# Low-rank products of an RWKV-7 mixer: half-height weights against full-height weights padded with zeros

## The chip, the cores and the metric

The kernel runs on one core of a Trainium2 chip. The metric is the device time of one execution in microseconds (us), as the median of three runs. A difference counts from about 0.2% (2.1 us) on.

## The reference, cut to what matters

One layer of a hybrid decoder: RMSNorm, one input projection of 512 tokens from 2048 to 7824 columns, three mixers side by side (RWKV-7, block attention, gated linear attention), an output projection, a residual and a last RMSNorm, all in float32. The change is in the RWKV mixer, in the two low-rank products that make the decay and the in-context rate of every token:

```python
r, k, v, wd, ad = _split(p, RWKV_SHIFT_SIZES)      # wd, ad: (512 tokens, 64)
w = w0 + jnp.tanh(wd) @ w2                          # w2: (64, 1024)
w = -jax.nn.softplus(-w) - 0.5
decay = jnp.exp(-jnp.exp(w))
a = jax.nn.sigmoid(a0 + ad @ a2)                    # a2: (64, 1024)
```

The contraction is over 64. The result is 1024 columns wide, in eight tiles of 128 (a tile is a pair of heads).

## The kernel before, in words

TensorE's fast float32 type (float32r) keeps fewer bits than float32. The kernel therefore splits an operand into a part hi, rounded to float32r, and a rest lo, and adds up several products. The input projection takes for each tile of 128 output columns 16 blocks of 128 input columns, and for each block three products of 128x128 weights with 512 tokens: hi by h hi, hi by h lo, lo by h hi (line 120, function mmr). They go to the four PSUM banks gb. A unit is four blocks, so 12 products. Its weights are loaded by SyncE's DMA queue into one of three buffers raw, rounded by ScalarE into hi (line 173) and subtracted by VectorE into lo (line 133), up to three units ahead of TensorE. The output projection is built in the same way.

Everything else (the three mixers) is side work: Python generators, resumed between the products of the projection when a rough model of the engines' queues says that their operands are there. That fixes, at build time, one order of instructions for each engine. The side work uses four other PSUM banks, sb.

The low-rank products are in `pair_decay`, called eight times, once for each pair of heads. The tokens' side is stored split on both halves of the 128 partitions: `wd` has tanh's hi part in partitions 0 to 63 and its lo part in 64 to 127, and `ad` has the lo part in 0 to 63 and the hi part in 64 to 127. The weights' side has w2's columns (and a2's) on both halves. So one 128-row product `w2hi` by `wd` gives hi·hi + hi·lo. What is left, the weights' lo part by the tokens' hi part, is a product over 64 rows: partitions 0 to 63 for the decay, 64 to 127 for the rate. Both lo parts share one tile, `w2lo`. Then ScalarE takes the sigmoid of each bank into `s0` (named vT in the profile) and `s2` (part of scr).

Tiles near it: `wl2` holds the split weights of the job "low" (16 columns of the gated linear attention's gate) and 96 columns of zeros behind them, since every "low" product reads 128 columns from its own place. `stat` and `rst` are small tiles with sums of squares and inverse roots, used at the start and in the last norm; `gn` holds the group norm's statistics of the RWKV mixer.

Of the kernel before, what the change touches and what calls it, by code (L numbers as in the profile page):

```python
# [9 lines left out]
F32 = mybir.dt.float32  # L10
F32R = mybir.dt.float32r
# [14 lines left out]
# first columns of the parts of w_in  # L26
# [4 lines left out]
# columns of the per-partition parameters  # L31
P_NW, P_MU, P_W0, P_A0, P_KK, P_KA, P_RK, P_LW, P_LB, P_GB, P_GN = 0, 16, 41, 49, 57, 65, 73, 81, 89, 97, 99
NPAR = 100
# columns of the constants
# [4 lines left out]
# the tiles of 128 columns of the input projection, in the order in which they are computed  # L39
# [22 lines left out]
class Clock:  # L62
    """A rough model of the engines' queues, used only to choose the order of emission."""
# [29 lines left out]
def tile_hybrid(ctx: ExitStack, tc: tile.TileContext, x, xT, wu, wlow, wout, par, cst, w2a2_d, aup_d, fw, out):  # L93
# [8 lines left out]
    def sb(name, shape, dt=F32, tag=None):  # L102
        t_ = pool.tile(list(shape), dt, name=name, tag=tag or name)
        return t_
# [91 lines left out]
    stat = sb("stat", [128, 4, 4])  # L196
    rst = sb("rst", [128, 8])
    wd = sb("wd", [128, S], F32R)
    ad = sb("ad", [128, S], F32R)
    wl2 = sb("wl2", [128, KT * 32 + 96], F32R)  # L200
# [14 lines left out]
    # RWKV: four heads (two pairs) at a time  # L215
# [12 lines left out]
    gn = sb("gn", [128, 3, 16])  # L228
    pbuf = [sb(f"pbuf{i}", [128, S + 1]) for i in range(2)]
# [9 lines left out]
    # the parts that live where others have been used up  # L239
# [7 lines left out]
    # the lanes of the triangular solves, once the rest of the preparation is over  # L247
# [7 lines left out]
    # the transposed x, before the branches start  # L255
# [39 lines left out]
    def pump():  # L295
        """Resume the side work whose operands are there by now."""
        for s in list(sides):
            now = ck.t["pe"]
            if runnable(s) and s.ready + MARGIN <= now and ck.t["dve"] < now + BACKLOG and ck.t["act"] < now + BACKLOG:
                resume(s)  # L300
        sides[:] = [s for s in sides if not s.done]

    def force(flag, what):
        """Let the tensor engine wait until the side work has got to flag."""
        while not flag():
            ready = [s for s in sides if runnable(s)]
            if not ready:
                raise RuntimeError(f"stuck: {what}: {[s.name for s in sides]}")
            s = min(ready, key=lambda s: s.ready)
            ck.t["pe"] = max(ck.t["pe"], s.ready + MARGIN)  # L310
            resume(s)
            sides[:] = [s for s in sides if not s.done]
# [44 lines left out]
    def rsqrt(v, r, scale, e):  # L357
        """r = (v scale + e)^-1/2"""
        ts(v, v, scale, e, ALU.mult, ALU.add)
        n = numel(v)  # L360
        ck.add("pool", 0.1 + 0.17 * n)
        nc.gpsimd.tensor_tensor(r, v, mhalf[:, 0:n], op=ALU.pow)  # L362
        yield None
# [41 lines left out]
    def resets(t):  # L405
        """1, and 0 where a chunk starts"""
        ck.add("pool", 1.0)
        nc.gpsimd.memset(t, 1.0)
        nc.gpsimd.memset(t[:, 0:S:C], 0.0)
# [3 lines left out]
    def parts(src):  # L413
        """src in two parts that add up to it exactly, each of them float32r"""
        yield lambda: not lock[0]
        lock[0] = True
        act(xr[0], src, AF.Copy)
        tt(xr[1], src, xr[0].bitcast(F32), ALU.subtract)
        yield None

    def pair_decay(pr, j):
        resets(s4)
        act(w2hi, w2a2, AF.Copy)
        yield None
        tt(w2lo[0:64], w2a2[0:64, 0:128], w2hi[0:64, 0:128].bitcast(F32), ALU.subtract)
        tt(w2lo[64:128], w2a2[64:128, 128:256], w2hi[64:128, 128:256].bitcast(F32), ALU.subtract)
        if pr < 7:
            load_w2a2(pr + 1)
        yield None
        b = yield from bank()  # L430
        mmr(sbk[b], w2hi[:, 0:128], wd, True, False)
        mmr(sbk[b], w2lo[0:64], wd[0:64], False, True)
        act(s0, sbk[b], AF.Sigmoid, bias=col(P_W0, pr))
        release(b)
        b = yield from bank()
        mmr(sbk[b], w2hi[:, 128:256], ad, True, False)
        mmr(sbk[b], w2lo[64:128], ad[64:128], False, True)
        act(s2, sbk[b], AF.Sigmoid, bias=col(P_A0, pr))
        release(b)
        yield None  # L440
        ck.add("dve", 1.15)
        nc.vector.tensor_tensor_scan(s1, s4, s0, 0.0, ALU.mult, ALU.add)
        yield None
        act(Pb[:, :, 1:C + 1], s1.rearrange("p (c t) -> p c t", t=C), AF.Exp, scale=-DECAY)
        act(s0, s1, AF.Exp, scale=DECAY)
        yield None
# [63 lines left out]
    def a_stage(q, c):  # L510
        """the products within chunks c and c + 1; the two heads of a pair take different row tiles and so banks"""
        mi = mask_i[:, None, None, :].to_broadcast([128, 2, 2, C])
        ms = mask_s[:, None, None, :].to_broadcast([128, 2, 2, C])
        bs = yield from bank(2)
        pa, pb = (sbk[b].rearrange("p (c r n) -> p c r n", c=2, r=2) for b in bs)
        for i in range(2):
            for j in range(2):
                mm(pa[:, i, j], BK[0:64, c + i, j], AW[0:64, c + i, j, 0:2])
                mm(pb[:, i, j], BK[64:128, c + i, j], AW[64:128, c + i, j, 1:3])
        yield None  # L520
        cs = slice(c, c + 2)
        act(Lt[0:64, :, cs], pa[0:64, :, :, 0:64].rearrange("p c r t -> p r c t"), AF.Copy)
        act(Lt[64:128, :, cs], pb[64:128, :, :, 64:128].rearrange("p c r t -> p r c t"), AF.Copy)
        yield None
        flags[f"L{q}"] = flags.get(f"L{q}", 0) + 1
        tt(ARB[:, cs, :, 0], pa[:, :, :, 64:128], mi, ALU.mult)
        tt(AW[64:128, cs, :, 0], pa[64:128, :, :, 0:64], ms[64:128], ALU.mult)
        release(bs[0])
        yield None
        tt(ARB[:, cs, :, 1], pb[:, :, :, 0:64], mi, ALU.mult)  # L530
        tt(AW[0:64, cs, :, 2], pb[0:64, :, :, 64:128], ms[0:64], ALU.mult)
        release(bs[1])
        flags[f"A{q}"] = flags.get(f"A{q}", 0) + 1
        yield None
# [12 lines left out]
    def key_norms(q, j):  # L547
        """the squared norms of the unnormalised keys of a token, laid out as the lanes of solve()"""
# [25 lines left out]
    def solve():  # L574
        """Tt: -(diag(n2) + L)^-1, transposed; one diagonal block of 32 per lane, then the block beside them."""
# [55 lines left out]
    def y_pair(q, cp):  # L631
        """the mix of chunks 2 cp and 2 cp + 1, tokens on the partitions"""
# [23 lines left out]
    def chain(q):  # L656
# [3 lines left out]
        for c in range(NC):  # L660
# [22 lines left out]
            if c < NC - 1:  # L683
# [7 lines left out]
                if c >= 2:  # L691
                    # the state that is overwritten has been read
                    yield lambda: flags.get(f"ymm{q}", 0) > (c - 2) // 2
# [92 lines left out]
    def by_chunks(src, parts):  # L786
        """Transposes src: head h's columns of every chunk of tokens to the half h of the partitions."""
# [13 lines left out]
    def gla(g):  # L801
# [64 lines left out]
        vt = [fb[(4, 7)[i]].rearrange("p (c n) -> p c n", n=128) for i in range(2)]  # chunks 0 to 3, 4 to 7  # L866
# [64 lines left out]
    def moba(h):  # L931
# [5 lines left out]
        def window(w, p, pT):  # L937
            """128 queries: their scores, the softmax over the keys so far, its product with the values"""
# [112 lines left out]
    # the operands of the last pass take the place of the branches' tiles  # L1051
# [41 lines left out]
    def square(n, r):  # L1093
        """the sum of squares of x"""
# [35 lines left out]
    def advance(u):  # L1130
        """Emit the loads and splits for the units up to u."""
# [32 lines left out]
    nc.vector.tensor_copy(wl2[:, KT * 32:], att.rearrange("p a t -> p (a t)")[:, 0:96])  # L1164
# [79 lines left out]
    for cb in range(3):  # L1244
        banks = oldest if cb % 2 == 0 else sbk
        order = [(n, tb) for n in range(KT) for tb in range(4)]
        if cb == 0:
            # the bank of the input projection's last job comes last
            order[:8] = [(0, 0), (0, 1), (0, 2), (1, 0), (1, 1), (1, 2), (0, 3), (1, 3)]
# [17 lines left out]
    # the last columns: the blocks of tokens end one after the other  # L1267
# [5 lines left out]
    def scaled(tb):  # L1273
        """the rows of the block of tokens, times the inverse root of their mean square"""
# [28 lines left out]
def arrange(inputs):  # L1303
    """The arrays of the launch: the inputs, laid out for the loads, and constants that depend on shapes alone."""
# [22 lines left out]
    # for every pair of heads the columns of w2 and of a2, on both halves of the partitions  # L1327
# [29 lines left out]
```

## Time and profile before

| | |
|---|---|
| median of 3 runs | 1071.08 us (1071.03 to 1071.57) |
| span of the profiled execution, first to last instruction | 1069.9 us |
| TensorE (PE) busy | 1044.7 us, 98% of the span |
| VectorE (DVE), ScalarE (ACT), GpSimd (POOL) busy | 62%, 42%, 7% |
| share of PE in the chain of work that ended last | 89% |

The page gives no time of the profiled execution other than its span; the median of the runs lies 1.2 us above that span. PE's busy time adds up modelled ends of pipelined products (a 128x512 product is shown as 0.39 us while the next one begins 0.23 us after it), so the steps between starts tell more than the durations.

### The profile page before, as it was taken

What the parts mean: (1) busy time and instruction counts of PE and PEld (TensorE: products, weight loads), DVE (VectorE), ACT (ScalarE), POOL (GpSimd) and SP (SyncE); (2) the same over time, 40 slices, a digit from 0 to 9 for tenths busy, and PEclk for the clock granted to TensorE, in tenths of its full rate; (3) what the DMA queues carried; (4) which work ended last, traced back from release to release, by engine and by line L of the source; (5) the groups of instructions that cost most, each with busy time, mean ns of one, the idle gap of its engine ahead of it and who ended that gap; (6) DMA issues with size and microseconds to landing.
All of it is one profiled execution on the core that took longest, in us unless ns stands there. A gap on an engine that the chain in (4) does not pass through costs nothing.

```text
span 1069.9 us, 16750 instructions
## 1 busy us (share of the span) xinstructions
PE 1044.7 (98%) x6376; PEld 819.0 (77%) x6376; DVE 667.7 (62%) x1345; ACT 444.6 (42%) x789; POOL 71.9 (7%) x73
## 2 busy tenths in 40 slices
PE   7799999999999999999999999999999999899996
PEld 5577888767778886777887777788877787688885
DVE  6646669656856885676778665667955564434343
ACT  6464543343454433235534423545322354423333
POOL 4500000000100000000000001000000000102020
PEclk9899999999999999999999999999999999999999
DMA  7232333412233342223334222333341245543434
GB/s 248 94 90 86 89 89 99 108 57 83 80 104 90 100 113 71 70 82 112 94 94 118 66 70 74 85 98 100 105 103 51 80 148 168 177 154 94 164 119 157
DMA packets 80400, 111.87 MB, mean 105 GB/s; under 512 B 28208, under 2 KB 29424, under 8 KB 80192
## 3 DMA queue, kind: packets, MB, share of 16 engines
q1 hardware_dynamic: 80176, 109.76, 34.7%
q8 instruction: 50, 0.82, 0.3%
q0 software_dynamic: 144, 1.05, 0.3%
q14 instruction: 30, 0.25, 0.1%
HBM read 98.62 MB, written 12.16 MB: 104 GB/s over the span
## 4 chain that ended last, share of the span: by engine, by line
PE 89%; DMA 3%; DVE 2%; ACT 2%; issue 2%; POOL 2%; SPq 0%; ACTq 0%; POOLq 0%; DVEq 0%
PE gb L120 67%; PE sb L116 11%; PE sb L120 10%; PE sb L125 2%; POOL f L1103 2%; DVE scr L133 1%; DMA raw<-in_wout_dram 1%; DVE lo L133 1%; DMA raw<-mix 1%; ACT hhi L173 1%; DMA Ld<-Lt 0%; ACT hi L173 0%; DMA raw<-in_wu_dram 0%; ACT f L173 0%; DMA scr<-Ld 0%
## 5 line engine op out<-in xcount | busy, mean ns | idle before, releaser
L120 PE MATMUL gb<-hhi,hi 128*128 128x512 f32 x976 | 404.6, 415 | 6.3 <-ACT hi L173 6.3
L120 PE MATMUL gb<-hhi,lo 128*128 128x512 f32 x976 | 383.7, 393 | 0.8 <-DVE lo L133 0.8
L120 PE MATMUL gb<-hlo,hi 128*128 128x512 f32 x976 | 383.0, 392 | 0.0
L173 ACT ACTIVATE hi<-raw 128x512 fp32r<-128x512 f32 x296 | 186.1, 630 | 398.7 <-PE gb L120 274.7
L133 DVE TENSOR_TENSOR lo<-raw,hi 128x512 fp32r<-128x512 f32 x296 | 213.1, 723 | 213.4 <-ACT hi L173 210.3
L120 PEld LDWEIGHTS gb<-hhi,hi 128*128 128x128 f32 x976 | 184.3, 189 | 51.5 <-ACT hi L173 6.5
L120 PEld LDWEIGHTS gb<-hhi,lo 128*128 128x128 f32 x976 | 184.1, 189 | 42.0 <-DVE lo L133 1.9
L120 PEld LDWEIGHTS gb<-hlo,hi 128*128 128x128 f32 x976 | 184.7, 189 | 33.7 <-issue 1.0
L133 DVE TENSOR_TENSOR scr<-scr 64x30 f32<-64x30 f32 (+14 forms) x240 | 77.5, 323 | 7.2
L120 PE MATMUL gb<-hi,hhi 128*128 128x512 f32 x128 | 50.2, 392 | 2.4 <-ACT hi L173 2.4
L120 PE MATMUL gb<-lo,hhi 128*128 128x512 f32 x128 | 50.2, 392 | 0.4 <-DVE lo L133 0.4
L120 PE MATMUL gb<-hi,hlo 128*128 128x512 f32 x128 | 49.9, 390 | 0.0
L173 ACT ACT_TABLE_LOAD x34 | 43.6, 1283 | 1.0 <-DVE VS L153 0.4
L153 DVE COPY VS<-sb 64x128 f32<-64x128 f32 x64 | 18.5, 288 | 33.5 <-PE sb L116 32.4
L173 ACT ACTIVATE Lt<-sb 64x256 f32<-64x256 f32 (+1 forms) x64 | 19.3, 327 | 33.0 <-PE sb L116 30.4
L362 POOL TENSOR_TENSOR gn<-gn,mhalf 128x16 f32<-128x16 f32 x4 | 12.0, 2995 | 307.1 <-DVE gn L149 307.1
L173 ACT ACTIVATE f<-sb 64x256 f32<-64x256 f32 (+3 forms) x52 | 17.3, 363 | 35.9 <-PE sb L125 19.1
L120 PE MATMUL sb<-lo,hhi 128*128 128x512 f32 x80 | 31.2, 390 | 0.0
L120 PE MATMUL sb<-hi,hlo 128*128 128x512 f32 x80 | 31.2, 390 | 0.0
L120 PE MATMUL sb<-hi,hhi 128*128 128x512 f32 x80 | 31.2, 389 | 0.0
L120 PEld LDWEIGHTS gb<-hi,hhi 128*128 128x128 f32 x128 | 24.0, 188 | 8.1 <-ACT hi L173 3.2
L120 PE MATMUL sb<-late,hhi 128*128 128x512 f32 x96 | 30.0, 394 | 0.0
(229 smaller groups left out, 1145.8 us busy)
## 6 DMA issues: line engine op xcount, KB each, us to landing
raw<-in_wu_dram SPq DMA_DIRECT2D x244, 256.0 KB
raw<-in_wout_dram SPq DMA_DIRECT2D x64, 256.0 KB
raw<-mix SPq DMA_DIRECT2D x16, 256.0 KB
f<-in_x_dram SPq DMA_DIRECT2D x16, 256.0 KB
Ld<-Lt SPq DMA_DIRECT2D x4, 512.0 KB
mix<-f SPq DMA_DIRECT2D x8, 256.0 KB
mix<-ARB SPq DMA_DIRECT2D x8, 256.0 KB
AW<-in_xT_dram SPq DMA_DIRECT2D x6, 256.0 KB
```

What stands on the lines that cost most here:

```text
L116: nc.tensor.matmul(o, l, r, start=start, stop=stop)
L120: nc.tensor.matmul(o, l, r, start=start, stop=stop)
L125: nc.tensor.transpose(o, i, ident[:k, :k])
L133: nc.vector.tensor_tensor(o, a, b, op=op)
L153: nc.vector.tensor_copy(o, a)
L173: nc.scalar.activation(o, a, f, **kw)
L362: nc.gpsimd.tensor_tensor(r, v, mhalf[:, 0:n], op=ALU.pow)
L1103: nc.gpsimd.tensor_tensor(fb[0], fb[0], fb[1 + m % 3], op=ALU.add)
```

## The change

The lo part of a2 gets a place of its own, `a2lo`, the 128 columns behind the "low" weights in `wl2` (96 before). `w2lo` and `a2lo` are filled with zeros once, at the start, by two VectorE copies where there was one. Each pair then writes its lo parts into the same 64 partitions as before, so the other 64 stay zero, and the two lo products take all 128 partitions of weights and tokens. `stat` and `rst` now lie inside `gn`. Comments were removed. Apart from the one copy that is added on VectorE at the start, the instructions of all engines stand in the same order as before.

```diff
     wd = sb("wd", [128, S], F32R)
     ad = sb("ad", [128, S], F32R)
-    wl2 = sb("wl2", [128, KT * 32 + 96], F32R)
+    wl2 = sb("wl2", [128, KT * 32 + 128], F32R)
+    a2lo = wl2[:, KT * 32:KT * 32 + 128]
...
-    stat = sb("stat", [128, 4, 4])
-    rst = sb("rst", [128, 8])
...
     gn = sb("gn", [128, 3, 16])
+    stat = gn[:, 0].rearrange("p (t c) -> p t c", t=4)
+    rst = gn[:, 1, 0:8]
...
     def pair_decay(pr, j):
...
-        tt(w2lo[64:128], w2a2[64:128, 128:256], w2hi[64:128, 128:256].bitcast(F32), ALU.subtract)
+        tt(a2lo[64:128], w2a2[64:128, 128:256], w2hi[64:128, 128:256].bitcast(F32), ALU.subtract)
...
         mmr(sbk[b], w2hi[:, 0:128], wd, True, False)
-        mmr(sbk[b], w2lo[0:64], wd[0:64], False, True)
+        mmr(sbk[b], w2lo, wd, False, True)
...
         mmr(sbk[b], w2hi[:, 128:256], ad, True, False)
-        mmr(sbk[b], w2lo[64:128], ad[64:128], False, True)
+        mmr(sbk[b], a2lo, ad, False, True)
...
-    nc.vector.tensor_copy(wl2[:, KT * 32:], att.rearrange("p a t -> p (a t)")[:, 0:96])
+
+    for z in (a2lo, w2lo):
+        nc.vector.tensor_copy(z, att.rearrange("p a t -> p (a t)")[:, 0:128])
```

## Rows read from the trace of the kernel before

**Rows 1.** The page's busy time, share of the span and instructions.
```profile
PE 1044.7 (98%) x6376; PEld 819.0 (77%) x6376; DVE 667.7 (62%) x1345; ACT 444.6 (42%) x789; POOL 71.9 (7%) x73
```
**Rows 2.** Chain that ended last: start, length, engine, output, line, count.
```profile
929.92 43.52 PE sb L120 x192
```
**Rows 3.** Timeline, first pair: start, length, engine, line, operation, tiles [idle before <-releaser].
```profile
67.28 0.40 PE L120 MATMUL gb<-hhi,lo 128*128 128x512 f32 x1
67.28 0.19 PEld L120 LDWEIGHTS sb<-wd,w2hi 128*128 128x128 f32 x1
67.51 0.40 PE L120 MATMUL sb<-wd,w2hi 128*128 128x512 f32 x1
67.84 0.18 PEld L120 LDWEIGHTS sb<-wd,w2lo 64*128 64x128 f32 x1 [0.37 <-issue]
67.84 0.49 PE L120 MATMUL sb<-wd,w2lo 64*128 64x512 f32 x1
...
68.26 0.50 PE L120 MATMUL sb<-ad,w2hi 128*128 128x512 f32 x1
68.37 0.69 ACT L173 ACTIVATE vT<-sb,params 128x512 f32<-128x512 f32 x1 [1.63 <-PE sb L120]
...
68.69 0.50 PE L120 MATMUL sb<-ad,w2lo 64*128 64x512 f32 x1
...
69.12 0.50 PE L120 MATMUL gb<-hhi,hi 128*128 128x512 f32 x1
...
69.23 0.69 ACT L173 ACTIVATE scr<-sb,params 128x512 f32<-128x512 f32 x1 [0.17 <-PE sb L120]
69.46 0.39 PE L120 MATMUL gb<-hlo,hi 128*128 128x512 f32 x1
```
**Rows 4.** Instructions that touch w2lo: count, minimum/median/maximum ns, first and last start.
```profile
L120 PE MATMUL sb<-wd,w2lo x8: 492/492/502, 67.8 to 690.7; 64*128 64x512 f32 x8
...
L120 PE MATMUL sb<-ad,w2lo x8: 491/498/498, 68.7 to 691.5; 64*128 64x512 f32 x8
```
**Rows 5.** Timeline, third pair, which comes behind 64-row products.
```profile
220.85 0.50 PE L120 MATMUL gb<-hhi,hi 128*128 128x512 f32 x1
221.19 0.39 PE L120 MATMUL gb<-hlo,hi 128*128 128x512 f32 x1
...
222.13 0.50 PE L120 MATMUL sb<-wd,w2hi 128*128 128x512 f32 x1
...
224.17 0.39 PE L120 MATMUL gb<-hlo,hi 128*128 128x512 f32 x1
```
**Rows 6.** Timeline, the recurrence beside the third pair.
```profile
222.25 0.59 DVE L153 COPY VS<-sb 64x128 f32<-64x128 f32 x2 [0.73 <-PE sb L116]
...
225.35 0.45 PE L116 MATMUL sb<-VS,BKt 128*64 128x64 f32 x8
```
**Rows 7.** Timeline, eighth pair, with 128x128 products right behind it.
```profile
690.36 0.39 PE L120 MATMUL sb<-wd,w2hi 128*128 128x512 f32 x1
...
691.95 1.16 PE L116 MATMUL sb<-att,f 128*128 128x128 f32 x8
```
**Rows 8.** Who waited for whom: us in total, times, longest.
```profile
ACT hi L173 <- PE gb L120: 274.7, 142, 9.5
```
**Rows 9.** Timeline, VectorE at the start.
```profile
2.91 0.20 DVE L1164 CAST wl<-att 128x96 fp32r<-128x96 f32 x1
...
4.96 0.75 DVE L139 SCALAR_TENSOR_TENSOR hlo<-AW,params,hhi 128x512 fp32r<-128x512 f32 x1 [1.85 <-ACT hhi L173]
```
**Rows 10.** Windows: busy us (instructions) of each engine, PEclk, DMA share, GB/s.
```profile
900.00:920.00 20.00, 18.26 (x79) 14.31 (x77) 7.33 (x11) 7.41 (x12) 0.00 (x0) 1.00 0.63 199
```
**Rows 11.** Windows of PE alone, around the stretch at the lower clock.
```profile
40.00:42.00 2.00, 1.24 (x6) 0.50 0.00 0
...
46.00:48.00 2.00, 2.00 (x7) 0.50 0.00 0
48.00:50.00 2.00, 2.00 (x11) 0.92 0.04 12
```

## Prediction, made before the changed kernel ran

> **What bounds the kernel now.** I read the page first, then the chain that ended last, the waits, and then the timeline at each of the eight places that the change touches. The page has TensorE (PE) busy for 98% of the span [rows 1], but that figure adds up modelled ends that overlap, so it doesn't say whether PE runs at its pace. The distance between starts does. Where nothing disturbs it, the chain has 192 products of 128x512 in 43.52 us [rows 2], that is 0.227 us from one start to the next. This step is the unit of everything below. The other engines mostly wait for PE: ScalarE alone waits 274.7 us, in 142 places, for a product to be through with a weight buffer before it can write the next one [rows 8]. So in the input projection a step that PE saves is a step that the end comes earlier, unless something that is now just in time becomes late.
>
> The eight calls of the low-rank products are two half-height products each, from 67.8 us to 691.5 us [rows 4]. Look at the first call [rows 3]. The full-height product `w2hi` by `wd` starts 0.23 us after its predecessor, though it writes another bank with other weights; its weight load starts at 67.28 us, together with the product before it. Then the pace breaks. The load of `w2lo` (marked 64*128) doesn't start beside the product before it but together with its own product, after 0.37 us in which the load path stood idle for "issue", that is, for nothing that the profile shows. From start to start the trace has 0.33 us to the first lo product, 0.42 us to `ad` hi, 0.43 us to the second lo product, 0.43 us to the next main product (67.51, 67.84, 68.26, 68.69, 69.12), and 0.34 us to the one after it (69.46). Each change between 128 and 64 rows costs about 0.1 us on the step into it and as much on the step behind it; in the middle, where every step has both, it is 0.2 us. The columns that are streamed are 512 in all of them, so the half height buys nothing.
>
> The Trainium skill, "TensorEngine Tiling (Array Packing)", Key Properties, says that a change of the tiling mode, other than a change of the tile within a mode, drains TensorE. The trace agrees: four changes in a call, and 0.81 us over the undisturbed pace.
>
> **The change part by part.**
>
> *The two lo products take 128 rows.* Then all four products of a call, and the main products around them, have one height. I take 0.227 us for each step, as for the other full-height products: half of the weights being zero changes neither the 512 columns nor the 128 of the load. No row has a full-height product with such operands, but a full-height product into an sb bank is in rows 3 (`w2hi` by `wd`, a step of 0.23 us). The bounds of this unknown: 0.227 us from below, since no 128x512 product in the trace is closer to its predecessor, and from above the 0.43 us of now, which would mean no gain. I take the lower one, because the row of a full-height product into sb gives it.
>
> Per call, from the start of `w2hi` by `wd` to the second product behind the call:
> - Four calls (first, second, fourth, seventh) stand between main products. Five steps take 1.95 us (67.51 to 69.46) and would take 5 x 0.227 = 1.135 us: 0.815 us less each, 3.26 us.
> - Two calls (third, fifth) come directly behind small side products of another height. Five steps take 2.04 us (222.13 to 224.17) [rows 5]. The entry out of the small products stays: 0.34 us, as from 220.85 to 221.19 in the same rows. So 0.34 + 4 x 0.227 = 1.25 us: 0.79 us less each, 1.58 us.
> - Two calls (sixth, eighth) are followed by 128x128 products. Four steps take 1.59 us (690.36 to 691.95) [rows 7] and would take 0.91 us: 0.68 us less each, 1.36 us. The small products behind them no longer come out of a half-height one; by the 0.11 us of the step 69.12 to 69.46 that is up to 0.2 us more for the two, which I leave to the range.
>
> Sum: 3.26 + 1.58 + 1.36 = 6.2 us.
>
> *The zeros.* One more copy on VectorE at the start, and one a third wider. The old copy took 0.20 us [rows 9]; two of 128 columns are about 0.45 us together, 0.25 us more. VectorE stands idle for 1.85 us right behind, until ScalarE has the first part of h [rows 9]. So it costs nothing. Without that cover it would cost 0.25 us.
>
> *a2lo behind the "low" weights, and stat and rst in gn.* The last "low" products read 128 columns, so their tail now reads `a2lo` instead of zeros, into rows of the bank that nobody uses. In the order of the instructions these products stand between the first and the second call, so both the write before and the write after them have long distances. The group norm is through with `gn` before the output projection writes the sums of squares there. No new wait here; from 0 to 0.1 us.
>
> *What then comes late.* ScalarE's two sigmoids are 0.69 us each and stand 0.86 us apart [rows 3]. The first can start some 0.2 us earlier (0.1 us from the step, 0.1 us from a product shown as 0.40 instead of 0.49 us). The second then waits for the first, no longer for PE, and ends about 0.3 us earlier, while PE gets 0.8 us ahead. So ScalarE loses 0.5 us of its lead in each call. Its lead is up to three units of twelve products, 36 x 0.227 = 8 us, and it has idle time to make it up [rows 8]. Beside the third call runs the recurrence: VectorE's copies of VS end at 222.84 us, and the product that needs them starts at 225.35 us [rows 6]. Of these 2.5 us the call takes 0.8 us, so they still arrive in time. Between 900 and 920 us PE idles 1.7 us for data [rows 10]; the loads there are released by buffers that PE frees, so this stretch moves forward as a whole.
>
> From the span of the profiled execution, 1069.9 - 6.2 = 1063.7 us. The median of the runs is 1.2 us above that span, so the predicted time is 1064.9 us, 0.58% less. Measurement tells about 0.2% (2.1 us) from no change.
>
> **The rivals.**
>
> *The steps don't shrink.* The 0.43 us steps could belong to the four products and not to their height, for instance to changing weights and bank. Then the time stays at 1071.1 us. Against it stands the 0.23 us step into the first product of the call, which changes both. Half of it is possible: at 0.34 us for each of the 16 products in place of 0.227 us, 1.8 us of the gain are lost and the time is 1066.7 us.
>
> The Trainium skill has a rule by which it would come out this way: "TensorE: Matmul & The Clock Gate", Part 3, The mechanism, says that a weight load overlaps with a running product only when its row group differs. By that rule full-height loads would never overlap, each step would stay at some 0.42 us (a load of 0.19 us and a step of 0.23 us), and the time would be 1071.1 us. The trace disagrees: full-height loads start beside a running full-height product, and it is the half-height load that does not.
>
> *PE's lead is eaten.* If after each call PE had to wait for ScalarE, it would keep 0.3 of its 0.8 us, so 2.3 to 2.6 us in all, and the time is 1068.6 us. For it: the sigmoids do become a queue of two. Against it: ScalarE's long waits for PE.
>
> *Slower: the clock.* PE ran at the lower of its two levels (1.2 GHz, granted clock 0.50) from when it resumed in the slice of 40 to 42 us until the slice of 48 to 50 us [rows 11], behind the idle time at the start, which cost about 8 us x 0.5 = 4 us. The change shifts VectorE's first instructions and with them possibly that stretch, or a later one. It decides from 12.4 us of work at the lower level on, when it takes more than the 6.2 us. Two further stretches of 8 us would take 8 us: 1072.9 us. Against it: the idle time of rows 9 covers the shift, and nothing in the change makes PE idle.
>
> **How the numbers follow.** The forecast, with its part where a step is not fully won (1064 to 1067.2 us): 0.85. PE's lead eaten for the most part (1067.5 to 1069 us): 0.06, of which nearly all still counts as faster. Steps don't shrink, by whatever cause: 0.06. Slower: 0.03. Faster by over 0.2% is 0.85 + 0.05 = 0.90; within 0.2% 0.06 + 0.01 = 0.07; slower 0.03. The Trainium skill's rule on row groups is one such cause; I give it 0.02 of the 0.06. The range goes from 1063.9 us (6.4 us saved, and the 0.5 us by which runs of one kernel differ) to 1067.2 us (the steps half won, with the same scatter).
>
> **What would show it.** In the profile after, the four products of each call and the two main products behind them start 0.23 us apart, their loads are marked 128*128 and have no idle time of "issue" before them, and the first call is over by about 68.65 us instead of 69.46 us. The last call lies some 5.5 us earlier, and from there to the end the distance stays the same. The forecast is wrong if the steps stay above 0.3 us, if PE shows new waits for ScalarE in the 10 us behind a call, or if the slices at the lower clock change in number.

## The result, and the profile after

| | before | after |
|---|---|---|
| median of 4 runs each | 1071.05 us (1071.0 to 1071.57) | 1065.52 us (1063.7 to 1066.36) |
| span of the profiled execution | 1069.9 us | 1064.5 us |

The ratio is 0.995, with a 95% interval of 0.9936 to 0.9964. The forecast was 1064.9 us, 0.6 us under the median. Two further measurements, each beside the kernel before on its own chip, gave 0.9946 (0.9932 to 0.9961) and 0.9948 (0.9935 to 0.996).

The first call after, as the timeline shows it for TensorE and the weight loads of the two lo products (columns as in [rows 3], to which these rows answer; `a2lo` lies in `wl2` and is called wl in the profile):

```profile
67.06 0.39 PE L120 MATMUL sb<-wd,w2hi 128*128 128x512 f32 x1
67.06 0.19 PEld L120 LDWEIGHTS sb<-wd,w2lo 128*128 128x128 f32 x1
67.28 0.40 PE L120 MATMUL sb<-wd,w2lo 128*128 128x512 f32 x1
...
67.52 0.40 PE L120 MATMUL sb<-ad,w2hi 128*128 128x512 f32 x1
67.52 0.19 PEld L120 LDWEIGHTS sb<-ad,wl 128*128 128x128 f32 x1
67.72 0.69 ACT L173 ACTIVATE vT<-sb,params 128x512 f32<-128x512 f32 x1 [1.44 <-PE sb L120]
67.75 0.40 PE L120 MATMUL sb<-ad,wl 128*128 128x512 f32 x1
...
67.99 0.40 PE L120 MATMUL gb<-hhi,hi 128*128 128x512 f32 x1
...
68.22 0.39 PE L120 MATMUL gb<-hlo,hi 128*128 128x512 f32 x1
...
68.31 0.68 ACT L173 ACTIVATE scr<-sb,params 128x512 f32<-128x512 f32 x1
```

The lo products' loads are marked 128*128 and start beside the product before their own, and so do the other loads of the call; no idle time stands in brackets. The steps are 0.22, 0.24, 0.23, 0.24 and 0.23 us, 1.16 us in all where it was 1.95 us. The sigmoids now stand 0.59 us apart instead of 0.86, and the second follows the first without waiting.

The third call, and VectorE's copies beside it (they answer to [rows 5, 6]):

```profile
219.99 0.50 PE L120 MATMUL sb<-wd,w2hi 128*128 128x512 f32 x1
...
220.11 0.59 DVE L153 COPY VS<-sb 64x128 f32<-64x128 f32 x2 [0.72 <-PE sb L116]
220.33 0.39 PE L120 MATMUL sb<-wd,w2lo 128*128 128x512 f32 x1
...
221.25 0.40 PE L120 MATMUL gb<-hlo,hi 128*128 128x512 f32 x1
...
222.43 0.45 PE L116 MATMUL sb<-VS,BKt 128*64 128x64 f32 x8
```

From 219.99 to 221.25 us it is 1.26 us (2.04 before). The entry out of the smaller products keeps its 0.34 us. The copies end at 220.70 us and are needed at 222.43 us: 1.7 us to spare, where there were 2.5 us.

The eighth call (answers to [rows 7]) takes 0.93 us where it took 1.59 us:

```profile
683.87 0.39 PE L120 MATMUL sb<-wd,w2hi 128*128 128x512 f32 x1
...
684.80 1.05 PE L116 MATMUL sb<-att,f 128*128 128x128 f32 x8
```

Over all eight calls the same subtraction gives 0.79, 0.78, 0.78, 0.77, 0.79, 0.68, 0.79 and 0.66 us, 6.04 us. Within the 128x128 products behind the sixth and the eighth call another 0.06 and 0.11 us are gained (behind the eighth, 1.05 us in the row above where [rows 7] has 1.16 us).

VectorE's two copies of zeros at the start (answer to [rows 9]) take 0.22 us each, and 1.68 us of idle time follow:

```profile
2.87 0.22 DVE L1167 CAST wl<-att 128x128 fp32r<-128x128 f32 x1
3.01 0.22 DVE L1167 CAST w2lo<-att 128x128 fp32r<-128x128 f32 x1
4.91 0.75 DVE L139 SCALAR_TENSOR_TENSOR hlo<-AW,params,hhi 128x512 fp32r<-128x512 f32 x1 [1.68 <-ACT hhi L173]
```

**Where the lead was given back.** Since the order of TensorE's instructions is the same, the start of each product after can be subtracted from its start before. This lead is 0.51 us ahead of the first call (48.38 us before), 7.26 us behind the last (692.87 us before), and 5.4 us at the end. So the 7.26 us are not the calls' alone: 0.5 us stood there before them (see e1), and some 0.5 us more came between calls, 0.3 us of it at 563 us of the time before, where the kernel before waits for VectorE and the changed one doesn't. Of the 1.9 us that are lost behind the last call, 1.5 us are lost in the first pass of the output projection, where the lead falls from 6.9 to 5.4 us between 912 and 920 us of the time before. There the timeline after has (TensorE and its releasers, then the load that it waits for):

```profile
914.10 0.80 PE L120 MATMUL gb<-hi,hhi 128*128 128x512 f32 x1 [2.61 <-ACT hi L173]
914.82 0.80 PE L120 MATMUL gb<-lo,hhi 128*128 128x512 f32 x1
915.42 0.63 PE L120 MATMUL gb<-hi,hlo 128*128 128x512 f32 x1
915.84 0.63 PE L120 MATMUL gb<-hi,hhi 128*128 128x512 f32 x1
...
917.54 0.39 PE L120 MATMUL gb<-lo,hhi 128*128 128x512 f32 x1
```
```profile
903.35 1.84 SPq L1243 DMA_DIRECT2D f<-in_x_dram  x4
...
905.29 0.38 SPq L1090 DMA_DIRECT2D raw<-mix  x1
...
912.70 0.63 ACT L173 ACTIVATE hhi<-raw 128x512 fp32r<-128x512 f32 x1 [4.78 <-DMA raw<-mix]
```

And before, at the same place:

```profile
919.51 0.51 PE L120 MATMUL gb<-hi,hhi 128*128 128x512 f32 x1 [1.74 <-ACT hi L173]
```

Four loads of x (256 KB each, for the residual) are issued in one go. The load of a mixer's output behind them is issued at 905.29 us, and ScalarE can use it at 912.70 us, after 4.78 us of waiting. TensorE then stands idle for 2.61 us, not 1.74 us. The next two products follow VectorE's lo parts, which are there at 914.77 and 915.37 us (steps of 0.72 and 0.60 us); from 915.42 to 917.54 us they start 0.42 us apart and not 0.23: the granted clock is 0.53 between 914 and 916 us and 0.62 from 916 to 918 us, the lower of the two levels (1.2 GHz) for part of the time. Between 903 and 909 us it had been 1.00.

### The profile page after: what moved, and what is told of

Its sections match the earlier page's. It is cut to its first block, busy times and chain, and to the rows that moved or that the text cites. A ratio compares the mean times of both kernels' runs of the same rounds, so it can differ in the third digit from the quotient of the medians.

```text
span 1064.5 us, 16752 instructions
## 1 busy us (share of the span) xinstructions
PE 1039.1 (98%) x6376; PEld 819.9 (77%) x6376; DVE 667.2 (63%) x1346; ACT 443.7 (42%) x789; POOL 71.9 (7%) x73
## 3 DMA queue, kind: packets, MB, share of 16 engines
q0 software_dynamic: 144, 1.05, 0.3%
## 4 chain that ended last, share of the span: by engine, by line
PE 90%; DMA 3%; ACT 2%; POOL 2%; issue 2%; DVE 1%; SPq 0%; ACTq 0%; POOLq 0%
PE gb L120 68%; PE sb L116 11%; PE sb L120 9%; PE sb L125 2%; DMA raw<-in_wout_dram 2%; POOL f L1104 2%; DMA raw<-mix 1%; ACT hi L173 1%; ACT hhi L173 1%; DMA BK<-Xd 0%; DVE hlo L133 0%; DMA raw<-in_wu_dram 0%; DVE lo L133 0%; ACT f L173 0%; SPq L1243 0%
## 5 line engine op out<-in xcount | busy, mean ns | idle before, releaser
L363 POOL TENSOR_TENSOR gn<-gn,mhalf 128x16 f32<-128x16 f32 (+1 forms) x5 | 13.0, 2603 | 309.5 <-DVE gn L149 309.5
```

## Experiments

The kernel before was run with each batch on the same chip. Its median was 1069.71 us with e1 to e4, 1069.09 us with e5 to e8, 1069.2 us with e9 to e11; times of different batches compare by their ratio to it.

**e1: everything but the height.** The two products take 64 rows again, the rest stays as in the changed kernel.

```diff
-        mmr(sbk[b], w2lo, wd, False, True)
+        mmr(sbk[b], w2lo[0:64], wd[0:64], False, True)
...
-        mmr(sbk[b], a2lo, ad, False, True)
+        mmr(sbk[b], a2lo[64:128], ad[64:128], False, True)
```

> Zeros, the new place of a2's lo part, stat and rst inside gn, as in the changed kernel, but both lo products over 64 rows as before. Theory (the gain is the change of height, four times a call): no gain from all that, 1071 us, within 0.7 us; steps of 0.33, 0.42, 0.43, 0.43, 0.34 us in the first call. Rival (part of the gain comes from the layout or from the start, since the changed kernel was 0.5 us ahead before its first call): 1070.5 us or less, and the same lead of 0.5 us before the first call.

Measured: 1069.68 us, ratio 0.9998 (0.9989 to 1.0007). By its microseconds alone this would fit the rival (1070.5 us or less), but the kernel before took 1069.71 us on that chip, so the ratio decides. The steps of the first call are those of before: 67.07, 67.40, 67.83, 68.25, 68.68, 69.02. The lead before the first call is 0.47 us here too, as the rival had it, but it brings no gain in the median. It does not come from the layout. The windows of TensorE alone that answer to [rows 11], first of the changed kernel, then of its variant e11 (below):

```profile
46.00:48.00 2.00, 2.00 (x10) 0.72 0.00 0
```
```profile
46.00:48.00 2.00, 2.00 (x13) 1.00 0.01 4
```

Before, there were 7 products at a granted clock of 0.50 in this slice. Where the clock rises earlier, more products are done: the lead ahead of the first call is 0.51 us after and 1.50 us in e11. In e1 the slice has 10 products at 0.73; in e10, which is the changed kernel once more, it has 7 at 0.50 and the lead is 0.03 us. So this lead differs between executions of one kernel. The zeros and the new places give nothing that can be measured; the height gives the gain.

**e2: the changed kernel once more.** No edit.

> The changed kernel once more. Theory (PE is 6.7 us ahead at the last call in every execution, and 0 to 2 us are given back in the first pass of the output projection, by a wait for loads and a clock that falls in some executions): times between 1063.5 and 1066.5 us, and the lead at the last call the same within 0.6 us. Rival (the executions differ already in the calls or at the start): the lead at the last call differs by as much as the times.

Measured: 1063.55 us (1062.32 to 1066.16), ratio 0.9946. The lead at the last call is 6.65 us (7.26 us in the first profile), of which 0.66 us stood before the first call. At the last call the two differ by 0.61 us, where at most 0.6 us were expected; what each call gains differs by no more than 0.01 us, and the rest lies in waits of the side work between the calls. This profiled execution gives nothing back: in the first pass the longest wait is 1.09 us, the clock is 1.00, and the span is 1061.8 us. So the calls are alike, the first pass differs, and so do, by some tenths of a microsecond, the start and the side work's waits.

**e5: one product of two.** Only w2's lo product takes 128 rows.

```diff
-        mmr(sbk[b], a2lo, ad, False, True)
+        mmr(sbk[b], a2lo[64:128], ad[64:128], False, True)
```

> The changed kernel with a2's lo product over 64 rows again (w2's over 128): two changes of height in a call, not four. Theory (each change costs 0.2 us, half on the step into the product and half on the step behind it): steps of 0.23, 0.23, 0.33, 0.43, 0.34 us in the first call, 0.41 us per call more than the changed kernel, 3.2 us in eight calls; 1066.8 us beside the 1063.55 us of e2. Rival (the loss comes from two half-height products in one call that use different rows, so that one alone is free): steps of 0.23 us and the time of e2.

Measured: 1066.73 us, ratio 0.9976 (0.9967 to 0.9986), a little under half of the gain. The timeline of TensorE in its first call:

```profile
66.76 0.39 PE L120 MATMUL sb<-wd,w2hi 128*128 128x512 f32 x1
66.99 0.40 PE L120 MATMUL sb<-wd,w2lo 128*128 128x512 f32 x1
67.23 0.40 PE L120 MATMUL sb<-ad,w2hi 128*128 128x512 f32 x1
67.55 0.50 PE L120 MATMUL sb<-ad,wl 64*128 64x512 f32 x1
67.98 0.50 PE L120 MATMUL gb<-hhi,hi 128*128 128x512 f32 x1
68.32 0.39 PE L120 MATMUL gb<-hlo,hi 128*128 128x512 f32 x1
```

0.23, 0.24, then 0.32 into the half-height product, 0.43 out of it and 0.34 behind: the steps that were expected, and 1.56 us for a call, 0.40 us more than 1.16. One half-height product alone costs its two changes.

**e7: the same cost put somewhere else.** In the value stage, which has eight calls too, the second product with the block-diagonal ones takes 64 rows.

```diff
-        for i in range(2):
-            mmr(sbk[b], blockd, xr[i], i == 0, i == 1)
+        mmr(sbk[b], blockd, xr[0], True, False)
+        mmr(sbk[b], blockd[0:64], xr[1][0:64], False, True)
```

> The changed kernel with one new half-height product in another place: in the value stage (eight calls) the second of two products with the block-diagonal ones takes 64 rows. It leaves out the lo parts of the sum for one head of the pair. Theory (the loss belongs to the change of height, wherever it is): steps of 0.33, 0.43 and 0.34 us where the changed kernel has 0.23 us, 0.41 us in each of the eight calls, 1066.8 us beside the 1063.55 us of e2. Rival (it belongs to the low-rank products or to their place): no more than 0.3 us slower than e2.

Measured: 1066.14 us, ratio 0.9973 (0.9962 to 0.9984); against the changed kernel's 0.9946 that is 0.27%, 2.9 us. Its timeline in the second of those calls (TensorE's products and the half-height load; the block-diagonal ones lie in the tile that the profile calls sel):

```profile
170.57 0.40 PE L120 MATMUL gb<-hhi,lo 128*128 128x512 f32 x1
...
170.80 0.81 PE L120 MATMUL sb<-xr,sel 128*128 128x512 f32 x2
171.12 0.18 PEld L120 LDWEIGHTS sb<-xr,sel 64*128 64x128 f32 x1 [0.36 <-DVE scr L133]
...
171.55 0.50 PE L120 MATMUL gb<-hhi,hi 128*128 128x512 f32 x1
...
171.88 0.40 PE L120 MATMUL gb<-hlo,hi 128*128 128x512 f32 x1
```

The half-height load starts 0.32 us behind the product before it, the main product 0.43 us behind that, and the next 0.33 us later. VectorE is named as the releaser of the first gap, but the gap of 0.36 us is as long as that of "issue" in [rows 3] (0.37 us). The loss goes where the half height goes.

**e6: the two half-height products side by side.** Both banks are taken first; order hi, hi, lo, lo.

```diff
-        b = yield from bank()
+        b, b2 = yield from bank(2)
         mmr(sbk[b], w2hi[:, 0:128], wd, True, False)
-        mmr(sbk[b], w2lo, wd, False, True)
+        mmr(sbk[b2], w2hi[:, 128:256], ad, True, False)
+        mmr(sbk[b], w2lo[0:64], wd[0:64], False, True)
+        mmr(sbk[b2], a2lo[64:128], ad[64:128], False, True)
...
```

> Half-height lo products as before, but ordered hi, hi, lo (partitions 0 to 63), lo (64 to 127), in two banks that are taken together; the order of the side work around moves with it. Theory (a change between 128 and 64 rows costs, a change between the two halves doesn't): two changes of height in a call; steps of 0.23 us between the hi products, 0.33 us into the first lo, at most 0.23 us from lo to lo, 0.43 us to the next main product, 0.34 us behind it: 0.4 us over the undisturbed pace per call, about 1066.5 us. Rival (any change of the rows that are used costs): 0.43 us from lo to lo too, 0.6 us per call, 1068.5 us.

Measured: 1089.31 us, ratio 1.0186 (1.0173 to 1.02). Neither theory has this time. The steps in a call are right for the first one, and better from lo to lo: 0.23, 0.32, 0.01, 0.42, 0.34 us. But to wait for two banks changed the order of the side work: TensorE has waits for VectorE and ScalarE in the projection that the changed kernel has not, among them 8.0 us for VectorE's evacuation into pbuf, and two more stretches at the lower clock level (0.50 between 148 and 150 us and between 762 and 766 us). As a test of the whole time it failed, so it was repeated:

**e9: the same, with the side work's order kept.** The model of the queues is fed as in the changed kernel; only the two middle products of each call change places.

```diff
-        mmr(sbk[b], w2lo, wd, False, True)
...
+        for o, w, t in ((b, w2hi[:, 0:128], wd), (b2, w2hi[:, 128:256], ad)):
+            nc.tensor.matmul(sbk[o], w, t, start=True, stop=False)
+        for o, w, t in ((b, w2lo[0:64], wd[0:64]), (b2, a2lo[64:128], ad[64:128])):
+            nc.tensor.matmul(sbk[o], w, t, start=False, stop=True)
...
```

> The ordering of e6 (hi, hi, lo over partitions 0 to 63, lo over 64 to 127), but with the side work's order kept as in the changed kernel, so that only the two middle products of a call change places. In e6 the two half-height products started 0.01 us apart, and a call's five steps took 1.32 us, where the changed kernel takes 1.16 us and the kernel before 1.95 us. Theory (e6's 1089 us come from the other order of the side work, not from the products): 0.16 us per call, 1.3 us in all, slower than e10 of this batch, and 4.5 to 5.5 us faster than before. Rival (products that run side by side in two banks cost time elsewhere): slower than e10 by more than 4 us.

Measured: 1065.01 us, ratio 0.9962 (0.9949 to 0.9976); 0.95 us slower than the changed kernel in the same batch (e10), which the intervals alone don't tell from nothing, but far from the rival's 4 us. It is 4.2 us faster than before, where 4.5 to 5.5 us were expected. The timeline of its first call:

```profile
67.34 0.39 PE L449 MATMUL sb<-wd,w2hi 128*128 128x512 f32 x1
...
67.57 0.40 PE L449 MATMUL sb<-ad,w2hi 128*128 128x512 f32 x1
67.89 0.18 PEld L451 LDWEIGHTS sb<-wd,w2lo 64*128 64x128 f32 x1 [0.36 <-issue]
67.90 0.49 PE L451 MATMUL sb<-wd,w2lo 64*128 64x512 f32 x1
...
67.90 0.49 PE L451 MATMUL sb<-ad,wl 64*128 64x512 f32 x1
...
68.32 0.50 PE L120 MATMUL gb<-hhi,hi 128*128 128x512 f32 x1
...
68.66 0.39 PE L120 MATMUL gb<-hlo,hi 128*128 128x512 f32 x1
```

Two half-height products over different partitions, into different banks, start together. The call takes 1.32 us, 0.16 us more than the changed kernel's 1.16 us and 0.63 us less than before. A change from one half of the rows to the other costs nothing here; the change of height does, once in and once out.

Height is not the only thing whose change costs. The timeline of before has, among the full products, groups of small ones whose weights have all 128 rows but 64 columns (marked 128*64):

```profile
218.28 0.40 PE L120 MATMUL gb<-hhi,lo 128*128 128x512 f32 x1
218.61 0.45 PE L116 MATMUL sb<-VS,BKt 128*64 128x64 f32 x8
218.99 0.50 PE L120 MATMUL gb<-hhi,hi 128*128 128x512 f32 x1
219.33 0.40 PE L120 MATMUL gb<-hlo,hi 128*128 128x512 f32 x1
```

The step into the group is 0.33 us, and the one behind the first full product after it 0.34 us, as around the half-height products.

**e3, e4: the x loads four blocks later.** The give-back was to be tested: the changed kernel (e3) and e1 (e4), with the four x loads of the first pass at block 12.

```diff
-                load_x(cb)
+                if cb:
+                    load_x(cb)
+            if cb == 0 and n == 12 and tb == 0:
+                load_x(0)
```

> The changed kernel with the four loads of x for the first quarter of the residual issued four blocks later in the first pass of the output projection (at block 12 and not 8), behind all loads of the mixers' outputs. Theory (these 1 MB delay the load of a mixer's output that PE then waits for): PE's wait of 2.6 us there and the fall of the clock behind it go, the time is 1062 to 1063.2 us and the times lie closer together than 1 us. Rival (the loads are late by the three buffers, not by the x loads): the wait stays and the time is 1065 us as in the changed kernel.

> The kernel of e1 (half-height lo products) with the x loads four blocks later. Theory: the products' gain doesn't depend on that place, so this kernel is 6.2 to 6.8 us slower than e3, and 1.0 to 2.0 us faster than e1 (the wait of 1.7 us there goes). Rival (the wait of before absorbed nothing of the half-height products, and the give-back is bound to the faster kernel): as slow as e1.

Measured: e3 1062.32 us (1061.25 to 1065.29), ratio 0.9936 (0.9921 to 0.9951); e4 1070.0 us, ratio 1.0003 (0.9994 to 1.0012). The median of e3 lies in the expected range, but the spread is 4 us, not under 1 us, and e4 gained nothing where 1 to 2 us were expected. Beside e2 and e1 on the same chip, neither is clear of noise. The trace of e3 says why. The long wait at the old place is gone, and new ones stand at the seam to the second pass, with a fall of the clock behind them; e4 has the same (1.36 and 1.11 us of waiting, then a clock of 0.59 and 0.56 from 936 to 940 us). The timeline of e3, TensorE, ScalarE and VectorE, then a window (busy us with instructions of each engine, PEclk, DMA share, GB/s):

```profile
922.75 0.63 ACT L173 ACTIVATE hi<-raw 128x512 fp32r<-128x512 f32 x1 [3.27 <-DMA raw<-in_wout_dram]
...
928.28 3.89 DVE L133 TENSOR_TENSOR lo<-raw,hi 128x512 fp32r<-128x512 f32 x3 [1.78 <-ACT hi L173]
928.30 0.50 PE L120 MATMUL sb<-hi,hhi 128*128 128x512 f32 x1 [0.88 <-ACT hi L173]
929.93 0.50 PE L120 MATMUL sb<-lo,hhi 128*128 128x512 f32 x1 [1.13 <-DVE lo L133]
```
```profile
932.00:934.00 2.00, 2.00 (x7) 1.54 (x6) 0.60 (x2) 0.63 (x1) 0.00 (x0) 0.50 0.56 165
```

So the theory of e3 was half right: without the burst the long wait at the old place goes, but moved as one burst it gains nothing, since TensorE waits at the seam. These new waits are of another kind. The releasers are ScalarE and VectorE, which have the residual to do there; of VectorE's three subtractions two take 1.59 and 1.77 us while GpSimd multiplies, and the third 0.68 us. The changed kernel's VectorE is as slow at its seam (three in 3.9 us from 929.51 us), and TensorE doesn't wait. That the burst had used up the lead which covers this, by ScalarE's wait of 3.27 us for a weight load just before, is argued from the trace and not shown by a run.

**e8, e11: one x load per block.** At blocks 8 to 11, in the changed kernel.

```diff
-                load_x(cb)
+                if cb:
+                    load_x(cb)
+            if cb == 0 and 8 <= n < 12 and tb == 0:
+                t_ = n - 8
+                nc.sync.dma_start(fb[t_], x[128 * t_:128 * t_ + 128, 0:512])
```

> The changed kernel with the four x loads of the first pass of the output projection issued one per block, at blocks 8 to 11. Theory (it is the burst of four loads in one go, 1 MB, that makes PE wait, at block 12 in the changed kernel and at the seam between the passes in e3): no wait over 1 us of PE in the first pass nor at the seam, 1060 to 1062 us. Rival (the sum of the loads is too much for the buffers at any spacing): PE waits over 1.5 us in the first pass or at the seam, 1062.3 to 1064 us as e2 and e3.

> The changed kernel, beside e9 and e11 on one chip. All theories: 0.994 to 0.996 of the time of the kernel before.

> The kernel of e8 (one load of x per block) once more, beside the changed kernel on one chip. Theory (the burst of four loads costs 1 to 3 us in the first pass of the output projection): 1 to 3 us faster than e10. Rival (e8 and e2 differ by chip and chance): within 0.7 us of e10.

Measured: e8 1061.97 us, ratio 0.9929 (0.9916 to 0.9941), and no wait of TensorE over 0.23 us in the first pass or at the seam, nor in e11. On one chip the changed kernel (e10) took 1064.06 us, ratio 0.9948, and the spread version (e11) 1060.69 us, ratio 0.9918 (0.9904 to 0.9931): 3.4 us less, a little over the 1 to 3 us that were expected. TensorE's windows there (busy us and instructions, PEclk, DMA share, GB/s), first of e10, then of e11:

```profile
900.00:920.00 20.00, 18.24 (x75) 1.00 0.61 202
```
```profile
900.00:920.00 20.00, 19.55 (x85) 1.00 0.66 214
```

Ten more products in the same 20 us, 2.3 us of work. This version beats both kernels: 0.82% under the kernel before. Part of the 3.4 us between the two is not the loads' doing: the profiled e11 was 1.50 us ahead of the kernel before when it came to the first call, e10 only 0.03 us, by the clock at the start (see e1). The first pass alone tells more: the same 158 products (from 900 to 940 us in the kernel before) take 40.0 us before, 41.3 us in the first profile after, 39.1 and 39.2 us in e2 and e10, 39.8 us in e3, and 36.8 and 37.0 us in e8 and e11. So in these profiles the spread loads are worth 2.2 us or more beside the changed kernel.

## Why the prediction was right

- **The cause.** The prediction put the loss on changes between 128 and 64 rows, 0.1 us on the step in and 0.1 us on the step behind, four times a call. e5 (half of the changes, half of what the calls gain), e7 (the same loss made elsewhere) and e9 (a change of half without a change of height is free) show it; e1 excludes the layout.
- **The sum.** 6.2 us were forecast; the calls give 6.04 us (the step that it took as 0.227 us is 0.23 us), and 0.17 us come in the small products behind the sixth and eighth, which the prediction had put at up to 0.2 us. Two of its readings were off without harm: its lower end of 1063.9 us should be 1064.2 us by its own terms, and a 128x512 product does start sooner than 0.227 us behind a smaller one (0.03 us at 48.38 us before), which the sum does not use.
- **The rule on row groups.** The forecast weighed the Trainium skill's rule ("TensorE: Matmul & The Clock Gate", Part 3, The mechanism) that loads overlap only with products of another row group. Here full-height loads overlap with full-height products, 0.23 us apart, and what doesn't overlap is the load behind a change of height. The same section of the Trainium skill also lets a load go ahead into a background weight buffer, which the prediction left out; no run here shows such a buffer as such. What Part 3 of the Trainium skill's page says beside it, that products in different row groups run side by side, is what e9 shows, with both starts at 67.90 us.
- **The covers.** Zeros at the start: 0.44 us against 0.20 us, with 1.68 us of idle time behind, as forecast. The recurrence beside the third call kept 1.7 us of its 2.5 us. No new waits for ScalarE stand behind the calls: in the 10 us behind each, TensorE has no gap over 0.1 us.
- **What was missed.** "This stretch moves forward as a whole" was said of the loads in the output projection, and that the distance stays the same from the last call on. In the profiled execution it did not: 1.9 us of the lead were lost, 1.5 us of them in the first pass, to a longer wait and a fall of the clock, while e2 and e10 lost nothing there. By the prediction's own sign, a changed number of slices at the lower clock, this spoke against it; its clock rival had a later stretch, but from a shift at the start and not from a wait for loads. The range took this in by chance; the sum had no term for it. It had none for the start either, where the lead came out between 0.03 and 0.66 us in three profiles of the same kernel, and it put the scatter of runs at 0.5 us, where both kernels' times spread by 2 to 4 us on one chip in the later batches. So that the median lies only 0.6 us over the forecast is in part luck. How much of the 0.6 us comes from the first pass is not shown: one of the four executions was profiled.

## What to carry to other kernels

Here a product over half of the array's rows was no cheaper than one over all of them, and between full-height products it cost about 0.4 us more (e5: 1.56 us against 1.16 us for a call): in [rows 3], e7 and e9 the weights behind a change of height are loaded only when their own product starts. Fill the other rows with zeros, or put the half-height products next to each other, on different halves and in different banks. When TensorE gets ahead, look at the next burst of loads in its way: spreading four of them over four blocks was worth 2.2 us or more, a third of what the change itself gives.

## What was not expected of the hardware

- Two half-height products on different halves, in two banks, started within 0.01 us of each other, so together they took the time of one (e6, e9).
- Weights of full height and half width (128*64) broke the pace of the full products as much as half height did: 0.33 us into them and 0.34 us behind the first full product after them.
- The granted clock fell to 0.50 behind a wait of 2.61 us (after) and behind two of 0.88 and 1.13 us that stood close together (e3, 932 to 934 us). It stayed at 1.00 behind waits of 1.74 us (before), 1.09 us (e2), and 0.48 and 0.60 us (e10).
- To ask for two PSUM banks at once, in a kernel whose order is planned by a model, cost 24 us beside e9, which has the same products in the planned order (ratios 1.0186 and 0.9962), through other waits and two more stretches at the lower clock.
